# Weight tiles in one address class modulo 256 bytes, with the first MLP projection's weight parts at sixteen different distances from it

## The chip, the core and the metric

The kernel runs on one core of one Trainium2 chip. The metric is the time of one execution of the whole program in microseconds (us), measured on the device. The profile is of one such execution. Engines are named as in the profile: PE is the matrix engine (TensorE), PEld its weight loads, DVE the vector engine, ACT the scalar engine, POOL the GpSimd engine, SP the engine whose queue issues most of the loads.

## The reference

One layer of a decoder trunk on a sequence of 256 positions and a width of 2048, all in fp32:

```
h   = RMSNorm(x)
proj = h @ w_in                      # (256, 2048) @ (2048, 15376), split into branch inputs
oa  = gated delta rule               # branch A, 8 heads, chunks of 64
ob  = HGRN2 gated recurrence         # branch B, 8 heads
oc  = cross-attention into 256 memory tokens (mem_n @ w_kv_mem)   # branch C
merged = sum_b sigmoid(G_b h) * (o_b @ W_br_b)
x   = x + RMSNorm(merged @ w_out)
h2  = RMSNorm(x)
x   = x + RMSNorm(relu(h2 @ w_mlp_in)^2 @ w_mlp_out)              # width 8192 between
```

Most of the work is dense matrix products of 256 rows of activations with weights that are read once from HBM, 357 MB in all.

## The kernel before

**Split products.** fp32 accuracy is reached with a reduced fp32 type of the matrix engine (F32R): each operand is split into a high part and a low remainder, and a product becomes three: high by high, high by low, low by high. Weights arrive in 512 KB pieces of 256 rows by 512 columns (2 tiles of 128 rows, `KG = 2`); in each SBUF partition a piece is 4096 bytes. ACT copies a piece into a high part (`wh` or `oh`), DVE subtracts to give the low part (`wl` or `ol`), and PE uses both. ACT and DVE therefore do one instruction of about 1.05 and 1.22 us per piece, and PE reads every weight from where these two wrote it.

**Two ways to multiply.** In a *plain unit* (`unit`, and the products of `seven`) the activations are the stationary operand (128 columns are loaded into the array) and the weights are the moving one: for each 128-row tile and each of two halves of the positions there are three matmuls of 512 columns, which move `wh`, `wl`, `wh`. In a row of the profile such a matmul is `mm<-wl,hh`: first the moving tile, then the stationary one. In a *stacked unit* (`unit_stacked`, for all of the first MLP projection but its first unit; `unit_joined` in the layer's first part) the weights are stationary in blocks of 128 columns, and the activations move: a wide matmul moves 512 columns (high and low activations side by side) past the high weights, a narrow one moves 256 columns past the low weights (`mm<-h2h,oh` and `mm<-h2h,ol`). A stacked unit takes its 8 pieces two at a time: 16 wide and 16 narrow matmuls for each two, in alternating order; 64 and 64 in all.

**Where the tiles lie.** Until the end of `w_out` the weights come from the pool `wp`: four buffers each for the raw piece, for `wh` (4096 bytes each) and for `wl` (4224 bytes each, that is 128 more than 4096). After that, in the MLP, `pair_at` makes six pairs `oh0`/`ol0` to `oh5`/`ol5`, with `oh` of 4096 and `ol` of 4224 bytes, and `operand` hands them out in turn. The helper `low` places the low part in its tile, 16 floats (64 bytes) from the start where `aside` is true, which it is in the joined and stacked units.

Call a tile's byte address in its partition modulo 256 its *class*. All activations that PE reads in the products of weights (`hh`, `h2h`, `memT`, `mh`, `ml`, `sh`, `sl`, `mgh`, ...) lie in class 128. So do all `wh`. The `wl` of `wp` alternate between 128 and 0 from buffer to buffer, since 4224 is 16.5 times 256; in joined units, with their 64 bytes, between 192 and 64. The pairs of the MLP alternate too: `oh0`, `oh2`, `oh4` with their `ol` lie in class 128, `oh1`, `oh3`, `oh5` with theirs in class 0; the low parts of stacked units lie 64 bytes on, in classes 192 and 64. In this document the *distance* is the class of the weight minus the class of the activation, which is always 128: it is 0 or 128 for most tiles, and 64 or 192 (that is, minus 64) for the low parts of joined and stacked units.

**What sets the order.** Instructions are issued in the order of the code on each engine, with background steps of other branches put between groups by `tick`. The MLP runs over `e` from 0 to 7: a projection `mlp_in(e)` of two units (`u` 0 and 1, `c0 = e * 1024 + u * 512`, so `c0 // 512` counts the sixteen units), then `mlp_out(e - 1)`, which uses seven products in place of eight (`seven`) and two plain units; `mlp_out_last` ends the kernel with four plain units.

Of the kernel before, what the change touches and what calls it, by code (L numbers as in the profile page):

```python
# [11 lines left out]
F32R = mybir.dt.float32r  # L12
# [5 lines left out]
P = 128  # L18
# [15 lines left out]
KG = 2  # L34
# [6 lines left out]
def tile_trunk(ctx: ExitStack, tc, a):  # L41
# [44 lines left out]
    wp = weights.enter_context(tc.tile_pool(name="wp", bufs=4, side="right"))  # L86
# [3 lines left out]
    def nm(s):  # L90
        cnt[0] += 1
        return f"{s}_{cnt[0]}"

    def g4(name, shape=(P, 1024), dt=F32):
        return gp.tile(list(shape), dt, tag="g", name=nm(name))
# [11 lines left out]
    def bank(name):  # L107
        return pbp.tile([P, 512], F32, tag="bp", name=nm(name))
# [79 lines left out]
    def tick(share=1.0):  # L188
        credit[0] += rate[0] * share
        n = int(credit[0])  # L190
        credit[0] -= n
        pump(n)
# [9 lines left out]
            ))  # L202
        return w

    def low(t, aside):
        o = 16 if aside else 0
        return t[:, o:o + KG * 512].rearrange("p (k n) -> p k n", k=KG)

    def split_w(w, n, width=512, step=None, q=lambda i: i, home=None, aside=False):
        if home:  # L210
            wh, wl = home(aside)
        else:
            wh = wp.tile([P, KG, 512], F32R, tag="wh", name=nm("wh"))
            wl = low(wp.tile([P, KG * 512 + 32], F32R, tag="wl", name=nm("wl")), aside)
        for j in range(0, n, step or n):
            js = slice(j, min(j + (step or n), n))
            q(A.copy(wh[:, js, 0:width], w[:, js, 0:width]))
            q(V.tensor_tensor(out=wl[:, js, 0:width], in0=w[:, js, 0:width],
                              in1=wh.bitcast(F32)[:, js, 0:width], op=ALU.subtract))
        return wh, wl  # L220
# [36 lines left out]
    def products_joined(ps, groups, nk, cs, turned):  # L257

        for wide in (0, 1) if turned else (1, 0):
            for k0, (wh, wl), both in groups:
                for c in cs:
                    for j in range(KG):
                        end = k0 + j == nk - 1 and wide == turned
                        if wide:
                            T.matmul(ps[c], wh[:, j, c * P:(c + 1) * P], both[j], start=k0 + j == 0, stop=end)
                        else:
                            T.matmul(ps[c][:, 0:S], wl[:, j, c * P:(c + 1) * P], both[j][:, 0:S], start=False, stop=end)  # L270
                yield

    def flat(b):
        return b.rearrange("p s n -> p (s n)")

    def unit_stacked(pairs, nk, src, c0, ps, load, ws):

        for gg in range(0, nk // KG, 2):
            groups = []
            for g in (gg, gg + 1):  # L280
                k0 = g * KG
                groups.append((k0, ws[g] if g in ws else load(src, k0, c0, True),
                               [flat(pairs[kt // 4][:, kt % 4]) for kt in range(k0, k0 + KG)]))
            for i, _ in enumerate(products_joined(ps, groups, nk, range(4), gg // 2 % 2)):
                tick(0.5)
# [75 lines left out]
    def load_mem(g):  # L361

        c, half = g // 2, g % 2
        memB.append(g4("memT", (P, 2, 2, S), F32R))
        if half == 0:
            mem_s.append(g4("mem", (P, NT, 512)))
        if c < 2:
            sl = slice(half * 256, half * 256 + 256)
        elif half == 0:
            sl = slice(0, 512)  # L370
        else:
            return
        pin(nc.sync.dma_start(mem_s[c][:, :, sl], mem_r[:, :, c * 512 + sl.start:c * 512 + sl.stop]))
# [7 lines left out]
    def first_unit(src, c0):  # L381


        both = pmm.tile([P, 1024], F32, tag="mm", name=nm("mm"))
        ng = KT // KG
        ws, sw = {}, {}

        def fetch(g):
            load_mem(g)
            ws[g] = load_w_raw(src, g * KG, KG, c0, step=1 if g < 2 else None, q=pin)  # L390

        def piece(g, js, q=lambda i: i):
            if g not in sw:
                sw[g] = (wp.tile([P, KG, 512], F32R, tag="wh", name=nm("wh")),
                         low(wp.tile([P, KG * 512 + 32], F32R, tag="wl", name=nm("wl")), False))
            wh, wl = sw[g]
            q(A.copy(wh[:, js, :], ws[g][:, js, :]))
            q(V.tensor_tensor(out=wl[:, js, :], in0=ws[g][:, js, :], in1=wh.bitcast(F32)[:, js, :], op=ALU.subtract))

        def turn(g):  # L400
            parts = []
            for kt in (g * KG, g * KG + 1):
                pt, kk = bank("tr"), kt % 4
                for t in range(NT):
                    pin(T.transpose(pt[:, t * P:(t + 1) * P], mem_s[g // 2][:, t, kk * P:(kk + 1) * P], ident))
                parts.append((pt[:, 0:S], *mem_act(kt), gcol[:, kt:kt + 1]))
            return parts

        def products(kt):
            ah, al = mem_act(kt)  # L410
            wh, wl = sw[kt // KG]
            j = kt % KG
            ts = [slice(t * P, (t + 1) * P) for t in range(NT)]
            os = [both[:, t * 512:(t + 1) * 512] for t in range(NT)]
            for o, t in zip(os, ts):
                pin(T.matmul(o, ah[:, t], wh[:, j, :], start=kt == 0, stop=False))
                pin(T.matmul(o, al[:, t], wh[:, j, :], start=False, stop=False))
            for o, t in zip(os, ts):
                pin(T.matmul(o, ah[:, t], wl[:, j, :], start=False, stop=kt == KT - 1))

        fetch(0)
        fetch(1)
        idle_turns(11)
        turn_grow(grow_mem, 16, 0, pin)
        split_scaled(turn(0), pin)
        idle_turns(8)
        for j in range(KG):
            piece(0, slice(j, j + 1), pin)
        for g in range(ng):
            if 1 <= g < ng - 1:  # L430
                piece(g + 1, slice(0, KG))
            if g + 2 < ng:
                fetch(g + 2)
            products(g * KG)
            if g == 0:
                for j, part in enumerate(turn(1)):
                    split_scaled([part], pin)
                    piece(1, slice(j, j + 1), pin)
            elif g + 1 < ng:
                split_scaled(turn(g + 1))  # L440
            products(g * KG + 1)
            if g % 2 == 0 and g > 0:
                sumsq_chunk(mem_s[g // 2 - 1], ssm, g // 2 - 1)
            tick()
        sumsq_chunk(mem_s[3], ssm, 3)
        return both
# [851 lines left out]
    for hg in range(2):  # L1298
        k, g = forget(unit_joined(hboth, w_in, OFF_BF + 512 * hg), hg)
        q = unit_joined(hboth, w_in, OFF_BQ + 512 * hg)  # L1300
# [75 lines left out]
    ahead = {}  # L1376

    def first_weights(ps):
        for g in range(2):
            ahead[g] = load_w(a["w_mlp_in"][0], g * KG, KG, 0,  # L1380
                              home=lambda aside: tuple(g4(n, (P, KG, 512), F32R) for n in ("wh", "wl")))

    for c in range(4):
        ys.append(g4("y1", (P, NT, 512)))
# [37 lines left out]
    def at(pool, tag, dt):  # L1422
        return pool.tile([P, KG, 512], dt, tag=tag, name=tag, bufs=1)

    def pair_at(pool, i):
        return at(pool, f"oh{i}", F32R), pool.tile([P, KG * 512 + 32], F32R, tag=f"ol{i}", name=f"ol{i}", bufs=1)

    pairs = [pair_at(wx, i) for i in range(2)]
    raws = [at(wx, "raw0", F32)]

    def wide_ring():
        for g in range(2):
            w = load_w_raw(a["w_mlp_in"][0], g * KG, KG, 512)
            ahead[8 + g] = split_w(w, KG, home=operand, aside=True)
        weights.close()
        wy = ctx.enter_context(tc.tile_pool(name="wy", bufs=1, side="right", reuse_waits="tile"))
        raws.extend(at(wy, f"raw{i}", F32) for i in range(1, 5))
        raws.append(g4("raw5", (P, KG, 512)))
        pairs.extend(pair_at(wy, i) for i in range(2, 6))

    def operand(aside):
        pairs.append(pairs.pop(0))
        return pairs[-1][0], low(pairs[-1][1], aside)

    def raw(src, k0, c0):
        w = raws.pop(0)
        raws.append(w)
        nc.sync.dma_start(w, src[k0 * P:(k0 + KG) * P, c0:c0 + 512].rearrange("(k p) n -> p k n", p=P))
        return w

    def load_in(src, k0, c0, aside=False):
        return split_w(raw(src, k0, c0), KG, home=operand, aside=aside)

    h2act = act_of(h2T)
    stf = const("stf", [P, 8])
# [240 lines left out]
```

## Time and profile before

| | |
|---|---|
| time, median of 3 runs (range) | 1783.41 us (1782.7 to 1784.26) |
| the profiled execution's own time | 1783.16 us |
| its span, first to last instruction | 1781.4 us |
| PE busy | 1767.7 us, 99% of the span |
| DVE busy | 1302.8 us, 73% |
| ACT busy | 961.1 us, 54% |
| granted PE clock | 0.999 |
| DMA | 362.84 MB, 204 GB/s mean |

The program has 8841 matmul instructions, and the trace shows a record for each (9053, since some plain fp32 matmuls run in two passes). Matmuls are pipelined: one that moves 512 columns has a record of about 0.39 us, but the next starts some 0.23 us later. So the time that PE needs for a stretch of work is read from the starts of its rows, not from their durations. The page's mean duration in a row of PE is not its pace.

The MLP begins at about 1101 us of the span. From there stages of the first projection (two units, 44.1 us) and of the second (41.6 to 43.2 us) alternate; the last second projection runs from 1687 to 1773 us.

### The profile page before, as it was taken

The numbers are of one execution on the slowest core, as the hardware profiler recorded it, in microseconds if no ns is written. First come the engines' busy times: TensorE is split into PE (matmuls) and PEld (weight loads), VectorE is DVE, ScalarE is ACT, GpSimd is POOL, SyncE is SP. The second block draws the span as 40 slices with busy tenths as digits, with TensorE's granted clock in tenths as the row PEclk, the third lists the DMA queues.
The fourth block names the chain that finished last, engine by engine and source line by source line (L and its number), as shares of the span: only waits on it lengthen the run. The fifth ranks groups of instructions, "written<-read, shape, count | busy, mean of one in ns | idle before, by whom it ended". The sixth has DMA issues, their size and how long they took to land.

```text
span 1781.4 us, 23962 instructions
## 1 busy us (share of the span) xinstructions
PE 1767.7 (99%) x9053; PEld 1491.5 (84%) x9053; DVE 1302.8 (73%) x1764; ACT 961.1 (54%) x1217; POOL 57.8 (3%) x100
## 2 busy tenths in 40 slices
PE   9999999999999999999999999999999999999998
PEld 7888888888888888888888888888888878888886
DVE  6865768684758487697555557796979797969795
ACT  7645666454555475565444445665545464646453
POOL 0000000400030000000000000000000000000000
PEclk9999999999999999999999999999999999999999
DMA  8665555865487465555666665776767676767683
GB/s 272 206 194 166 175 156 166 232 205 156 154 215 213 130 195 166 156 171 174 183 186 192 233 224 197 231 244 217 245 222 252 206 245 217 256 200 257 204 298 139
DMA packets 188804, 362.84 MB, mean 204 GB/s; under 512 B 14456, under 2 KB 16272, under 8 KB 188304
## 3 DMA queue, kind: packets, MB, share of 16 engines
q1 hardware_dynamic: 181856, 351.32, 61.9%
q0 software_dynamic: 2304, 5.44, 1.6%
q10 hardware_dynamic: 4528, 4.54, 0.9%
q8 instruction: 71, 1.16, 0.3%
q14 instruction: 45, 0.37, 0.1%
HBM read 356.86 MB, written 4.39 MB: 203 GB/s over the span
## 4 chain that ended last, share of the span: by engine, by line
PE 81%; DVE 2%; issue 1%; ACT 1%; DMA 0%; DVEq 0%; POOLq 0%; POOL 0%
PE mm L56 77%; DVE ol L56 1%; PE pa L56 1%; PE kk L56 0%; DMA raw<-in_w_mlp_out 0%; DVE relu L56 0%; PE bo L56 0%; PE o L56 0%; PE pzt L56 0%; PE pw L56 0%; PE tr L56 0%; DVE raw L56 0%; DVE ml L56 0%; PE y L56 0%; PE mgT L56 0%
## 5 line engine op out<-in xcount | busy, mean ns | idle before, releaser
L56 DVE TENSOR_TENSOR wl<-w,wh 128x1024 fp32r<-128x1024 f32 (+1 forms) x362 | 436.8, 1217 | 238.2 <-ACT wh L56 215.8
L56 ACT CAST wh<-w 128x1024 fp32r<-128x1024 f32 (+1 forms) x362 | 374.7, 1045 | 357.9 <-PE mm L56 293.3
L56 ACT CAST oh<-raw 128x1024 fp32r<-128x1024 f32 x288 | 299.1, 1051 | 278.2 <-PE mm L56 213.8
L56 DVE TENSOR_TENSOR ol<-raw,oh 128x1024 fp32r<-128x1024 f32 x288 | 342.9, 1219 | 98.5 <-ACT oh L56 66.2
L56 PE MATMUL mm<-wh,hh 128*128 128x512 f32 x1152 | 366.6, 393 | 0.0
L56 PEld LDWEIGHTS mm<-wh,hh 128*128 128x128 f32 x1152 | 216.0, 188 | 46.3 <-ACT wh L56 0.2
L56 PE MATMUL mm<-h2h,oh 128*128 128x512 f32 x960 | 227.7, 393 | 0.0
L56 PE MATMUL mm<-wl,hh 128*128 128x512 f32 x576 | 226.1, 392 | 0.0
L56 PEld LDWEIGHTS mm<-h2h,oh 128*128 128x128 f32 x960 | 178.5, 188 | 38.2
L56 PE MATMUL mm<-hh,wh 128*128 128x512 f32 x768 | 184.8, 392 | 0.7 <-ACT z L56 0.7
L56 PEld LDWEIGHTS mm<-hh,wh 128*128 128x128 f32 x768 | 140.6, 188 | 28.3 <-ACT z L56 0.9
L56 PE MATMUL mm<-ol,mh 128*128 128x512 f32 x372 | 146.4, 393 | 1.1 <-DVE ol L56 1.0
L56 PE MATMUL mm<-oh,mh 128*128 128x512 f32 x372 | 146.2, 393 | 0.0
L56 PE MATMUL mm<-oh,ml 128*128 128x512 f32 x372 | 145.2, 393 | 0.0
L56 PEld LDWEIGHTS mm<-wl,hh 128*128 128x128 f32 x576 | 108.3, 188 | 21.4
L56 PEld LDWEIGHTS mm<-h2h,ol 128*128 128x128 f32 x960 | 113.7, 188 | 3.2 <-DVE ol L56 0.7
L56 PE MATMUL mm<-h2h,ol 128*128 128x256 f32 x960 | 114.6, 277 | 0.5 <-DVE ol L56 0.5
L56 PEld LDWEIGHTS mm<-hh,wl 128*128 128x128 f32 x768 | 97.0, 188 | 3.4
L56 PE MATMUL mm<-hh,wl 128*128 128x256 f32 x768 | 99.6, 280 | 0.0
L56 PEld LDWEIGHTS mm<-ol,mh 128*128 128x128 f32 x372 | 69.9, 188 | 18.5 <-DVE ol L56 2.8
L56 PEld LDWEIGHTS mm<-oh,mh 128*128 128x128 f32 x372 | 69.9, 188 | 16.6 <-DVE acc L56 1.1
L56 PEld LDWEIGHTS mm<-oh,ml 128*128 128x128 f32 x372 | 69.8, 188 | 15.7
(363 smaller groups left out, 2208.2 us busy)
## 6 DMA issues: line engine op xcount, KB each, us to landing
w<-in_w_in SPq DMA_DIRECT2D x240, 512.0 KB, 4.2
raw<-in_w_mlp_out SPq DMA_DIRECT2D x170, 512.0 KB, 4.6
raw<-in_w_mlp_in SPq DMA_DIRECT2D x118, 512.0 KB, 4.8
w<-in_w_out SPq DMA_DIRECT2D x32, 512.0 KB, 4.3
w<-in_w_kv_mem SPq DMA_DIRECT2D x30, 512.0 KB, 4.7
w<-in_w_br_c SPq DMA_DIRECT2D x16, 512.0 KB, 3.6
w<-in_w_br_a SPq DMA_DIRECT2D x16, 512.0 KB, 4.4
w<-in_w_br_b SPq DMA_DIRECT2D x16, 512.0 KB, 3.6
```

The costliest lines, as they stand in the source:

```text
L56: ins = op(*args, **kwargs)
```

## The change

The instructions, their order on every engine, their waits and the DMAs are the same in both programs. Only addresses in SBUF differ.

- In `wp` a low part that isn't aside is moved by 32 floats (128 bytes) in every second buffer. All `wl` of plain units then lie in class 128, like `wh` and the activations: distance 0. The low parts of joined units stay where they were (classes 192 and 64).
- The tiles of the MLP's pairs are 4352 bytes (17 times 256) for both parts, so all twelve lie in class 128. In `mlp_out` and `mlp_out_last`, where no place is given, all parts are at distance 0.
- In the stacked units of the first projection each unit takes its own pair of shifts from `places`, in floats, for the high and the low part. Unit 0 isn't stacked and takes none. In bytes (high, low), for units 1 to 15: (0, 128), (32, 32), (224, 224), (16, 96), (240, 160), (8, 16), (248, 240), (4, 8), (252, 248), (48, 48), (208, 208), (0, 192), (0, 64), (0, 4), (0, 0). Read modulo 256, 224 is minus 32, 240 minus 16, and so on.
- The pools `wx` and `wy` grow by 128 to 256 bytes per tile, so raw tiles lie at other addresses, all still in class 128.

```diff
-    def low(t, aside):
-        o = 16 if aside else 0
+    def shifted(t, o):
         return t[:, o:o + KG * 512].rearrange("p (k n) -> p k n", k=KG)
 
+    low_turn = [0]
+
+    def low(aside):
+        t = wp.tile([P, KG * 512 + 32], F32R, tag="wl", name=nm("wl"))
+        odd = low_turn[0] % 2
+        low_turn[0] += 1
+        return shifted(t, 16 if aside else 32 * odd)
...
+    places = [(0, 0), (0, 32), (8, 8), (56, 56), (4, 24), (60, 40), (2, 4), (62, 60),
+              (1, 2), (63, 62), (12, 12), (52, 52), (0, 48), (0, 16), (0, 1), (0, 0)]
+
     def unit_stacked(pairs, nk, src, c0, ps, load, ws):
...
-                groups.append((k0, ws[g] if g in ws else load(src, k0, c0, True),
+                groups.append((k0, ws[g] if g in ws else load(src, k0, c0, places[c0 // 512]),
...
     def pair_at(pool, i):
-        return at(pool, f"oh{i}", F32R), pool.tile([P, KG * 512 + 32], F32R, tag=f"ol{i}", name=f"ol{i}", bufs=1)
+        return tuple(pool.tile([P, KG * 512 + 64], F32R, tag=f"{t}{i}", name=f"{t}{i}", bufs=1) for t in ("oh", "ol"))
...
-            ahead[8 + g] = split_w(w, KG, home=operand, aside=True)
+            ahead[8 + g] = split_w(w, KG, home=operand, place=places[1])
...
-    def operand(aside):
+    def operand(place):
         pairs.append(pairs.pop(0))
-        return pairs[-1][0], low(pairs[-1][1], aside)
+        return tuple(shifted(t, o) for t, o in zip(pairs[-1], place))
...
-    def load_in(src, k0, c0, aside=False):
-        return split_w(raw(src, k0, c0), KG, home=operand, aside=aside)
+    def load_in(src, k0, c0, place=None):
+        return split_w(raw(src, k0, c0), KG, home=operand, place=place)
```

More of the change, by code (lines that the diff above doesn't have):

```diff
@@ L203, in load_w_raw, with split_w @@
         return w
-    def low(t, aside):
-        o = 16 if aside else 0
+    def shifted(t, o):
         return t[:, o:o + KG * 512].rearrange("p (k n) -> p k n", k=KG)
-    def split_w(w, n, width=512, step=None, q=lambda i: i, home=None, aside=False):
+    low_turn = [0]
[4 more added lines that the diff above has]
+        return shifted(t, 16 if aside else 32 * odd)
+    def split_w(w, n, width=512, step=None, q=lambda i: i, home=None, aside=False, place=None):
         if home:
-            wh, wl = home(aside)
+            wh, wl = home(place or (0, 16 if aside else 0))
         else:
             wh = wp.tile([P, KG, 512], F32R, tag="wh", name=nm("wh"))
-            wl = low(wp.tile([P, KG * 512 + 32], F32R, tag="wl", name=nm("wl")), aside)
+            wl = low(aside)
         for j in range(0, n, step or n):
@@ L394, in piece @@
                 sw[g] = (wp.tile([P, KG, 512], F32R, tag="wh", name=nm("wh")),
-                         low(wp.tile([P, KG * 512 + 32], F32R, tag="wl", name=nm("wl")), False))
+                         low(False))
             wh, wl = sw[g]
@@ L1380, in first_weights @@
             ahead[g] = load_w(a["w_mlp_in"][0], g * KG, KG, 0,
-                              home=lambda aside: tuple(g4(n, (P, KG, 512), F32R) for n in ("wh", "wl")))
+                              home=lambda place: tuple(g4(n, (P, KG, 512), F32R) for n in ("wh", "wl")))
     for c in range(4):
```

## Prediction, made before the change was run

> **What bounds the kernel now.** I read the page's busy times first, then the chain of waits from the start of the MLP on.
>
> ```profile
> span 1781.4 us, 23962 instructions
> PE 1767.7 (99%) x9053; PEld 1491.5 (84%) x9053; DVE 1302.8 (73%) x1764; ACT 961.1 (54%) x1217; POOL 57.8 (3%) x100
> by line: PE mm L56 90.3%; DVE ol L56 3.4%; issue 2.2%; DMA raw<-in_w_mlp_out 1.2%; DVE relu L56 1.1%; DVE raw L56 0.6%; DVE ml L56 0.5%; ACT oh L56 0.4%; ACT junk L56 0.1%; DVE yacc L56 0.1%; PE mT L56 0.1%; POOL rsf L1622 0.1%; ACT relu L5
> ```
>
> PE is the bound nearly everywhere; in the MLP a few per cent of the chain go through DVE. A change that alters no instruction can only act through how fast the same instructions run, so I went to the timeline of PE and took the pace from the starts of rows. The tile in a row was matched with its address in the built program.
>
> The second projection, in its last stage, where the weights move (`oh`, `ol` first) past activations at class 128. The first ten matmuls read a pair in class 128, the next twelve one in class 0, the last twelve one in class 128 again:
>
> ```profile
> 1734.60 0.39 PE L56 MATMUL mm<-oh,ml 128*128 128x512 f32 x1
> ...
> 1736.87 0.40 PE L56 MATMUL mm<-oh,mh 128*128 128x512 f32 x1
> ...
> 1739.66 0.39 PE L56 MATMUL mm<-oh,mh 128*128 128x512 f32 x1
> 1739.89 0.40 PE L56 MATMUL mm<-ol,mh 128*128 128x512 f32 x1
> 1740.12 0.39 PE L56 MATMUL mm<-oh,ml 128*128 128x512 f32 x1
> 1740.36 0.39 PE L56 MATMUL mm<-oh,mh 128*128 128x512 f32 x1
> ...
> 1742.39 0.40 PE L56 MATMUL mm<-oh,mh 128*128 128x512 f32 x1
> ```
>
> Ten matmuls take 2.27 us, 227 ns each, at distance 0. Twelve take 2.79 us, 232.5 ns each, at distance 128. Then three take 0.70 us (233 ns) and the next nine 2.03 us (226 ns): after a disturbance the pace comes back within a few matmuls. So a wide matmul at distance 128 costs 5.5 to 6 ns more than one at distance 0.
>
> A plain unit of `w_out`: a group of twelve with its low part in class 0, then a group with it in class 128.
>
> ```profile
> 1007.37 0.39 PE L56 MATMUL mm<-wh,mgh 128*128 128x512 f32 x1
> 1007.60 0.40 PE L56 MATMUL mm<-wl,mgh 128*128 128x512 f32 x1
> 1007.83 0.39 PE L56 MATMUL mm<-wh,mgl 128*128 128x512 f32 x1
> ...
> 1010.12 0.39 PE L56 MATMUL mm<-wh,mgh 128*128 128x512 f32 x1
> ...
> 1012.84 0.39 PE L56 MATMUL mm<-wh,mgh 128*128 128x512 f32 x1
> ```
>
> The first takes 2.75 us, the second 2.72: four of the twelve move a low part, so each costs about 7 ns more in class 0.
>
> The first projection, from the middle of one of its stages; equal matmuls follow each other there, so their rows merge:
>
> ```profile
> 1560.69 3.80 PE L56 MATMUL mm<-h2h,ol 128*128 128x256 f32 x32
> 1564.32 7.55 PE L56 MATMUL mm<-h2h,oh 128*128 128x512 f32 x32
> 1571.71 3.80 PE L56 MATMUL mm<-h2h,ol 128*128 128x256 f32 x32
> ```
>
> 32 narrow ones take 3.63 us, 113.4 ns each, half of 226.8: at distances 64 and 192 they run clean. 32 wide ones take 7.39 us, 230.9 ns each, 4.2 above 226.7: half of them have their weights at distance 128. A narrow matmul at distance 0 is seen only elsewhere, in the attention's scores, where all operands lie in class 128:
>
> ```profile
> 169.76 0.28 PE L56 MATMUL sc<-ckh,cqh 128*128 128x256 f32 x1
> ...
> 171.20 0.63 PE L56 MATMUL mm<-hh,wh 128*128 128x512 f32 x2
> ```
>
> Twelve take 1.44 us, 120 ns each: for a narrow matmul distance 0 is the bad place, by 6.6 ns.
>
> One page bears on why wide and narrow differ. The Trainium skill (TensorE: Matmul & The Clock Gate, LDWEIGHTS) gives the time of a weight load in ns as its columns divided by 1.2, so 107 ns for 128 columns; by that, as an estimate, a load nearly fills a narrow matmul's 113 ns and any delay to it shows, while under a wide one it has 120 ns to spare. The 113 and 120 ns agree with that; they don't prove it.
>
> **The change part by part.** The sum is made against the profiled execution, 1783.16 us with a span of 1781.4, 0.25 us under the median of 1783.41.
>
> *Plain units.* The low parts that move, from the groups by line:
>
> ```profile
> L56 PE MATMUL mm<-wl,hh 128*128 128x512 f32 x576 | 226.1, 392 | 0.0
> L56 PE MATMUL mm<-wl,oh 128*128 128x512 f32 x128 | 50.3, 393 | 0.2 <-DVE wl L56 0.2
> L56 PE MATMUL mm<-wl,mgh 128*128 128x512 f32 x128 | 50.2, 392 | 0.0
> L56 PE MATMUL mm<-wl,och 128*128 128x512 f32 x64 | 25.1, 392 | 0.0
> L56 PE MATMUL mm<-wl,memT 128*128 128x512 f32 x64 | 22.6, 394 | 0.0
> ```
>
> These are 960, half of them in class 0: 480 x 7 ns = 3.4 us. Some of these matmuls stand at waits for ACT or DVE, where a faster pace only waits longer, so I take 3.1. The bounds are 2.5 and 3.8 (the clean matmuls after a disturbed one gain a little too).
>
> *Second projection.* Its matmuls and the stage that shows its other limit, the first columns of the second row being the stretch, its length and PE's busy time, the third busy time DVE's:
>
> ```profile
> L56 PE MATMUL mm<-oh,mh 128*128 128x512 f32 x372 | 146.2, 393 | 0.0
> L56 PE MATMUL mm<-oh,sh 128*128 128x512 f32 x112 | 44.6, 399 | 0.2 <-DVE relu L56 0.2
> 1428.04:1471.27 43.23, 42.37 (x182) 33.41 (x180) 41.61 (x46) 25.95 (x27) 0.00 (x0) 1.00 0.70 234
> 1687.12:1773.00 85.88, 85.88 (x373) 69.57 (x371) 69.42 (x82) 40.51 (x50) 0.54 (x1) 1.00 0.60 215
> ```
>
> Three products for each row make 3 x (372 + 112) = 1452 matmuls, half at distance 128: 726 x 5.9 ns = 4.3 us, and the three slow ones after each change of class about 0.4 more: 4.7. But in the six stages before the last, DVE is busy 41.6 of 43.2 us and PE waits there for it; what PE saves ahead of such a wait is given back in it. Each stage would save some 0.55 us, and about half of that comes ahead of its last wait: 5 x 0.28 = 1.4 lost. The last stage has no wait and keeps its 1.4. I take 3.3, with bounds 2.0 (every earlier stage held by DVE) and 4.7.
>
> *First projection.* 15 stacked units of 64 wide and 64 narrow. Now each costs 64 x 4.2 ns = 0.27 us above the clean pace, narrow ones next to nothing: 4.2 us in all. Afterwards every wide matmul stands at 0 or within 48 bytes of it, and no narrow one is sure of its clean place. No row shows a distance that isn't a multiple of 64, so I bound and interpolate. Wide: 0.3 ns (distance 0) to 5.8 (distance 128), on a straight line 1.2 ns at the ten units' mean distance of 22 bytes, 0.08 us a unit. Narrow: 6.6 ns at 0 and none at 64, so about 6 at 4 and 8 bytes, 5 at 16, 3.3 at 32 (and at 96, 128, taken as midway to the unknown), 1.6 at 48; over the ten units with both parts shifted 3.8 on average, 0.25 us a unit. Ten units cost 3.3 us. Of the five others two (low at 64 and 192) are clean; the three with low at 128, 4 and 0 cost 3.3, 6.3 and 6.6 ns x 64, together 1.0. Sum 4.4 against 4.2: 0.2 us lost. Bounds: 1.0 if shifts cost nothing beyond those three (a gain of 3.2), and 17.9 + 1.1 if every matmul of the ten units loses 14 ns, the most that the rows suggest, twice a low part's 7 ns (a loss of 14.8). DVE and ACT don't hold these stages: DVE's writes and reads at shifted addresses cost as before where `ol` already stands 64 bytes on.
>
> ```profile
> 1297.55:1341.64 44.09, 44.09 (x257) 38.66 (x256) 30.83 (x31) 19.53 (x24) 0.00 (x0) 1.00 0.66 214
> L56 DVE TENSOR_TENSOR wl<-w,wh 128x1024 fp32r<-128x1024 f32 (+1 forms) x362 | 436.8, 1217 | 238.2 <-ACT wh L56 215.8
> L56 DVE TENSOR_TENSOR ol<-raw,oh 128x1024 fp32r<-128x1024 f32 x288 | 342.9, 1219 | 98.5 <-ACT oh L56 66.2
> ```
>
> PE fills this stage to the end, DVE has 13 of 44 us free; that is the cover, and with it gone a shift that slowed DVE by 43% would set the stage.
>
> Joined units are untouched. Sum: 1783.16 - 3.1 - 3.3 + 0.2 = 1777.0 us.
>
> **The rivals.**
>
> *The odd distances eat the gain.* Every matmul of the ten shifted units loses 7 ns, wide and narrow: 10 x 128 x 7 = 9.0, with the three low parts 10.1, so 5.9 more than now against 6.4 saved: 1782.7. For it: 7 ns is the step that both kinds of matmul show. Against: wide matmuls find their pace again by themselves at distance 0, and a small shift is a small phase.
>
> *The odd distances cost more than all else saves.* A weight block shifted by 4 to 48 bytes collides with the activations' reads on every load, twice over, and the wide matmuls never settle: 14 ns on each of the 1280 matmuls, 14.8 us lost, 1783.16 - 6.4 + 14.8 = 1791.6. It decides from (6.4 + 4.2 - 1.1 + 3.6) / 1280 = 10.2 ns each. Nothing in the trace shows such a place, nor excludes it.
>
> *The small shifts are free.* Narrow and wide run clean at all but the worst places: 3.2 gained in the first projection, 1773.6.
>
> *DVE takes the second projection's gain.* If each of the six earlier stages is set by DVE, 2.0 us of the 3.3 remain, and with narrow matmuls at 6.6 ns in all ten units the first projection loses 2.1: 1783.16 - 3.1 - 2.0 + 2.1 = 1780.2, at the edge of no change.
>
> *Addresses don't matter.* The time stays at 1783.2; the differences by class would be of something that goes with the buffer, such as the phase of the loads. Against it stand the rows of two kinds of unit with the same step. The Trainium skill (SBUF — State Buffer, SBUF: two separate sides) says that among engines only the port pair of DVE and GpSimd contends and that PE waits on nobody; by that rule the change would do nothing. The rows above, 227 against 232.5 ns, speak against it for PE's own two reads.
>
> **How the numbers follow.** Forecast 0.45; small shifts free 0.13; shifts eat the gain 0.19; DVE takes it 0.07; addresses don't matter 0.03; shifts cost more 0.13. A difference of 0.2%, 3.6 us, is about what a measurement of this kernel tells from none. Faster by more than that: 0.45 + 0.13 = 0.58. Within it: 0.19 + 0.07 + 0.03 = 0.29. Slower: 0.13. The predicted time is that of the forecast, 1777.0. Its own range, from the bounds of plain units and second projection and a first projection between -1.5 and +2.5, is 1773.5 to 1780.5. The range for 8 in 10 goes from 1772.5, below the free case, over the two cases of no change to 1786, and leaves out most of the last case.
>
> **What would show it.** In the profile after, groups of twelve in plain units should all take 2.72 us, and the last second projection should fall from 85.9 to about 84.5 us: if not, the class isn't the cause. The stage at 1428 us should shorten by less than 0.55 us and DVE's waits grow: that shows the give-back. In the first projection the unit with shifts (0, 64) should run 64 wide matmuls at 226.7 ns and 64 narrow at 113.3, and the one with (0, 0) its narrow ones at 120. The ten others decide the result: I am wrong on the slow side if their wide matmuls run above 234 ns, or narrow ones above 120, and on the fast side if both stay at the clean pace.

## The result and the profile after

| | before | after |
|---|---|---|
| median of the runs on the same chip (range), us | 1784.25 (1782.7 to 1785.66) | 1780.45 (1779.05 to 1781.7) |
| profiled execution, us | 1783.16 | 1781.33 |
| its span, us | 1781.4 | 1779.6 |
| first part, to the start of the MLP, us | 1100.03 | 1097.81 |
| seven stages of the first projection, us | 332.73 | 336.67 |
| seven stages of the second projection, us | 338.60 | 335.03 |

The change makes the kernel faster by 0.22%, 3.8 us by the medians: the ratio is 0.9978, with a 95% interval of 0.9971 to 0.9985. The forecast, 1777.0 us, stood 6.2 us below the profiled execution that it was summed from. The two profiled executions differ by only 1.83 us, since that of before was among the faster of its kernel and that of after among the slower; the parts below are compared between these two, and the timed runs of single parts (further down) show the same balance.

The page of after, busy times:

```profile
span 1779.6 us, 23962 instructions
PE 1764.0 (99%) x9053; PEld 1495.0 (84%) x9053; DVE 1302.7 (73%) x1764; ACT 961.4 (54%) x1217; POOL 58.8 (3%) x100
L56 PE MATMUL mm<-h2h,ol 128*128 128x256 f32 x960 | 119.0, 281 | 0.4 <-DVE ol L56 0.4
```

The same row of the narrow matmuls on the page of before:

```profile
L56 PE MATMUL mm<-h2h,ol 128*128 128x256 f32 x960 | 114.6, 277 | 0.5 <-DVE ol L56 0.5
```

PE is still the bound, with 3.7 us less to do, although 960 narrow matmuls got 4.4 us dearer. Where that shows is told by the busy times in stretches of the MLP. First before: the first row is the first part, then the sum of the first projection's stages, then that of the second's (stretch, its length, then busy times; in a sum, the sum of the lengths first):

```profile
1.64:1101.67 1100.03, 1098.27 (x5673) 929.60 (x5674) 751.36 (x1180) 599.28 (x792) 55.76 (x88) 1.00 0.63 189
...
sum 332.73, PE 332.19 PEld 290.92 DVE 235.58 ACT 160.29 POOL 0.00; mean PE 47.46 PEld 41.56 DVE 33.65 ACT 22.90 POOL 0.00
...
sum 338.60, PE 337.23 PEld 270.93 DVE 311.46 ACT 200.39 POOL 0.54; mean PE 48.18 PEld 38.70 DVE 44.49 ACT 28.63 POOL 0.08
```

And after, with three stages whose rows before the prediction shows: one of the first projection, an early one of the second, and the last:

```profile
1.65:1099.46 1097.81, 1094.70 (x5674) 929.44 (x5674) 751.28 (x1180) 599.86 (x792) 56.68 (x88) 1.00 0.63 190
...
1296.91:1341.83 44.92, 44.92 (x258) 39.27 (x256) 31.52 (x31) 19.55 (x24) 0.00 (x0) 1.00 0.67 211
...
sum 336.67, PE 336.22 PEld 294.79 DVE 236.23 ACT 160.19 POOL 0.00; mean PE 48.03 PEld 42.11 DVE 33.75 ACT 22.88 POOL 0.00
...
1427.99:1469.73 41.74, 41.48 (x182) 33.55 (x180) 40.76 (x46) 26.04 (x27) 0.00 (x0) 1.00 0.73 242
...
1686.32:1771.16 84.84, 84.84 (x373) 69.48 (x371) 69.61 (x82) 40.48 (x51) 0.54 (x1) 1.00 0.62 217
...
sum 335.03, PE 333.11 PEld 270.78 DVE 310.83 ACT 200.23 POOL 0.54; mean PE 47.59 PEld 38.68 DVE 44.40 ACT 28.60 POOL 0.08
```

The first part gained 2.2 us and the second projection 3.6, as forecast in kind. The first projection, for which 0.2 us was allowed, lost 3.9: its stage of 44.09 us takes 44.92, and PE fills it in both. The three differences add up to -1.85 us; the spans differ by 1.8.

Plain units and the second projection now run at one pace. The timeline of PE after, twelve matmuls of a plain unit whose low part would have been in class 0, then twelve of the last second projection:

```profile
1005.54 0.39 PE L56 MATMUL mm<-wh,mgh 128*128 128x512 f32 x1
...
1008.26 0.39 PE L56 MATMUL mm<-wh,mgh 128*128 128x512 f32 x1
...
1724.76 0.39 PE L56 MATMUL mm<-oh,mh 128*128 128x512 f32 x1
...
1727.48 0.39 PE L56 MATMUL mm<-oh,mh 128*128 128x512 f32 x1
```

Both take 2.72 us, 227 ns a matmul; before there were groups of 2.75 and of 2.79.

The first projection after: unit 10 (48 and 48 bytes), unit 12 (0 and 192), unit 15 (0 and 0):

```profile
1477.25 7.63 PE L56 MATMUL mm<-h2h,oh 128*128 128x512 f32 x32
1484.72 3.95 PE L56 MATMUL mm<-h2h,ol 128*128 128x256 f32 x32
1488.50 7.60 PE L56 MATMUL mm<-h2h,oh 128*128 128x512 f32 x32
...
1563.29 7.46 PE L56 MATMUL mm<-h2h,oh 128*128 128x512 f32 x32
1570.59 3.93 PE L56 MATMUL mm<-h2h,ol 128*128 128x256 f32 x32
1574.36 7.46 PE L56 MATMUL mm<-h2h,oh 128*128 128x512 f32 x32
...
1667.72 4.00 PE L56 MATMUL mm<-h2h,ol 128*128 128x256 f32 x32
1671.56 7.44 PE L56 MATMUL mm<-h2h,oh 128*128 128x512 f32 x32
```

By the starts, unit 10 runs 32 wide ones in 7.47 us, 233.4 ns each, as slow as at distance 128. Unit 12 has settled wide ones, 7.30 us or 228.1 ns each, but its 32 narrow ones at 192 take 3.77 us, 117.8 ns each, where the prediction counted on 113.4. At distance 0 they take 3.84 us, 120.0 ns, as forecast. From the same kind of rows, all units (before, each had wide ones at 230.6 to 231.1, narrow ones at 113.5, and 0.28 to 0.31 us above the clean pace of 226.7 and 113.3; unit 1's waits are left out):

| unit: shifts in bytes | wide, ns | narrow, ns | above clean pace, us |
|---|---|---|---|
| 1: 0, 128 | 227.8 | 119.4 | 0.43 |
| 12: 0, 192 | 228.1 | 117.7 | 0.37 |
| 13: 0, 64 | 227.4 | 117.8 | 0.33 |
| 14: 0, 4 | 227.8 | 118.1 | 0.37 |
| 15: 0, 0 | 227.5 | 119.8 | 0.47 |
| 5: -16, 160 | 228.1 | 119.9 | 0.52 |
| 8 and 9: 4, 8 and -4, -8 | 232.4, 231.9 | 115.8, 117.6 | 0.52, 0.61 |
| 6 and 7: 8, 16 and -8, -16 | 230.8, 233.1 | 118.3, 119.5 | 0.59, 0.81 |
| 4: 16, 96 | 231.5 | 118.0 | 0.61 |
| 2 and 3: 32, 32 and -32, -32 | 233.0, 233.2 | 118.5, 117.3 | 0.74, 0.67 |
| 10 and 11: 48, 48 and -48, -48 | 233.3, 231.8 | 118.3, 116.8 | 0.74, 0.55 |

Together 8.3 us against 4.3 before: 4.0 more, which is the loss of the stages.

### The profile page after: what moved, and what is told of

Same layout as the page of the kernel before. It is cut to its first block, busy times and chain, and to the rows that moved or that the text cites. A ratio compares the mean times of both kernels' runs of the same rounds, so it can differ in the third digit from the quotient of the medians.

```text
span 1779.6 us, 23962 instructions
## 1 busy us (share of the span) xinstructions
PE 1764.0 (99%) x9053; PEld 1495.0 (84%) x9053; DVE 1302.7 (73%) x1764; ACT 961.4 (54%) x1217; POOL 58.8 (3%) x100
## 4 chain that ended last, share of the span: by engine, by line
PE 78%; DVE 4%; issue 1%; DMA 1%; ACT 1%; DVEq 0%; POOLq 0%; POOL 0%; ACTq 0%
PE mm L56 74%; DVE ol L56 2%; PE pa L56 1%; DMA raw<-in_w_mlp_out 1%; DVE relu L56 1%; DVE raw L56 1%; PE kk L56 0%; DVE ml L56 0%; PE bo L56 0%; PE o L56 0%; PE pzt L56 0%; PE pw L56 0%; PE tr L56 0%; PE y L56 0%; PE mgT L56 0%
## 5 line engine op out<-in xcount | busy, mean ns | idle before, releaser
L56 PEld LDWEIGHTS mm<-h2h,ol 128*128 128x128 f32 x960 | 117.7, 188 | 3.2 <-DVE ol L56 0.6
L56 PE MATMUL mm<-h2h,ol 128*128 128x256 f32 x960 | 119.0, 281 | 0.4 <-DVE ol L56 0.4
```

The lines of the kernel that those rows point to most:

```text
L56: ins = op(*args, **kwargs)
```

## The experiments

Two questions were open. Why do narrow matmuls at distances 64 and 192 no longer run clean? And what are the two gains worth by themselves? For the first, one theory says that the table's odd shifts, or what goes with them, are at fault, and a narrow matmul's pace follows from its own distance. The other says that the pace of a narrow matmul follows from the state in which the wide ones ahead of it leave the two streams of reads: wide ones that were still unsettled, at distance 128, let it run clean, and wide ones that had settled at distance 0 don't. (The traces show starts and addresses, not reads: that it is PE's reads that collide is how both theories picture it, and isn't shown.)

### One class for all, no table (e1_one_class)

The changed kernel with one place for every stacked unit, high part at 0 and low part at 64 bytes:

```diff
-    places = [(0, 0), (0, 32), (8, 8), (56, 56), (4, 24), (60, 40), (2, 4), (62, 60),
-              (1, 2), (63, 62), (12, 12), (52, 52), (0, 48), (0, 16), (0, 1), (0, 0)]
+    places = [(0, 16)] * 16
```

> The change without its table: every weight tile in the class of the activations, all stacked units with shifts (0, 64 bytes). Theory A (the distance of a matmul's own operands sets its pace): narrow matmuls stand at distance 64 as in half of the kernel before, so they run at 113.3 ns, the wide ones at 226.7 but for the first few; the fifteen stacked units lose 1.0 us against 4.3 before, and the kernel is some 3.3 + 3.1 + 3.3 = 9 to 10 us faster than before. Theory B (the pace hangs on the phase that the matmuls before leave; narrow ones run at 113 only when they follow wide ones that have not settled): narrow ones take 117.8 ns as in units 12 and 13 of the change, each unit loses 0.33 us, 5.0 in all, and the kernel is only 5 to 6 us faster than before.

Measured: 1778.88 us (1777.0 to 1779.17) against 1784.72, ratio 0.9963 (0.9949 to 0.9977). A stage of the first projection on its timeline, and the sum of the seven stages:

```profile
1118.47 7.44 PE L56 MATMUL mm<-h2h,oh 128*128 128x512 f32 x32
1125.75 3.93 PE L56 MATMUL mm<-h2h,ol 128*128 128x256 f32 x32
1129.52 7.44 PE L56 MATMUL mm<-h2h,oh 128*128 128x512 f32 x32
```

```profile
sum 333.35, PE 332.82 PEld 294.34 DVE 236.34 ACT 160.23 POOL 0.00; mean PE 47.55 PEld 42.05 DVE 33.76 ACT 22.89 POOL 0.00
```

With no odd shift anywhere, the wide ones run at 227.5 ns, and narrow ones at the very distance that was clean before take 3.77 us, 117.8 ns each. So the clean pace isn't a property of the distance alone. The first projection still stands 0.6 us above before, and the table costs 3.3 us more than a single place: without it the change would be worth some 6.6 us by this ratio (4.1 to 9.1), 5.8 by the medians.

### The last wide ones before each narrow run put at distance 128 (e4_unsettled)

As e1, but of a unit's eight pieces the second and the sixth have their high part moved by 128 bytes. Theirs are the wide matmuls just ahead of a run of narrow ones; all low parts stay at 64 bytes.

```diff
+    def place_of(g):
+        return (32 if g in (1, 5) else 0, 16)
...
-                groups.append((k0, ws[g] if g in ws else load(src, k0, c0, places[c0 // 512]),
+                groups.append((k0, ws[g] if g in ws else load(src, k0, c0, place_of(g)),
```

> As e1, but in each stacked unit the high parts of the second and sixth piece, after which narrow matmuls follow, stand at distance 128. Theory B: the wide matmuls of these two pieces take some 232.5 ns (0.05 us more for each piece), the narrow ones after them fall to 113.3 ns within four; a unit loses 0.15 to 0.18 us, 2.3 to 2.7 in all, and the kernel is 2.3 to 2.7 us faster than e1. Theory A: narrow ones run at the same pace as in e1, and the kernel is 1.4 us slower than e1.

Measured: 1777.19 us (1773.96 to 1778.68) against the runs of before, ratio 0.9951 (0.9939 to 0.9964), some 8.7 us faster than before by the ratio and 7.5 by the medians. The same stretch, and the sums of both projections:

```profile
1118.19 7.50 PE L56 MATMUL mm<-h2h,oh 128*128 128x512 f32 x32
1125.53 3.80 PE L56 MATMUL mm<-h2h,ol 128*128 128x256 f32 x32
1129.16 7.50 PE L56 MATMUL mm<-h2h,oh 128*128 128x512 f32 x32
```

```profile
sum 331.03, PE 330.54 PEld 290.80 DVE 236.02 ACT 160.09 POOL 0.00; mean PE 47.22 PEld 41.54 DVE 33.72 ACT 22.87 POOL 0.00
...
sum 334.91, PE 333.04 PEld 270.97 DVE 310.55 ACT 199.78 POOL 0.54; mean PE 47.58 PEld 38.71 DVE 44.36 ACT 28.54 POOL 0.08
```

Nothing about the narrow matmuls was changed, and they went from 117.8 to 113.4 ns (3.63 us for 32). The wide ones got slower by 1.9 ns (7.34 us for 32), and a unit stands 0.17 us above the clean pace, against 0.33. So what stands ahead of them sets their pace, as the theory of the state at entry has it, and the narrow one's own distance alone doesn't.

### Low parts at 64 and 192 in turn (e5_alternate)

The kernel before also had its low parts at 64 and 192 by turns. As e1, with that turn:

```diff
+    def place_of(g):
+        return (0, 48 if g % 2 else 16)
```

> As e1, but the low parts of the stacked units stand at distance 64 and 192 in turn from piece to piece, as in the kernel before; all wide matmuls at 0. It tells whether the turn between 64 and 192, and not the unsettled wide matmuls, kept narrow ones at 113 ns before. If the turn did it: narrow ones 113.4 ns throughout and 0.08 us above the clean pace for a unit. If the phase on entry does (theory B): narrow ones begin at 118 as in e1; as in the joined units, where the turn comes every four matmuls, a turn may shift the phase on the way, so 115 to 118 ns on average and 0.2 to 0.35 us for a unit.

A single execution gave 1779.85 us against 1784.86. Narrow ones stay at 117.8 ns:

```profile
1119.08 7.48 PE L56 MATMUL mm<-h2h,oh 128*128 128x512 f32 x32
1126.40 3.93 PE L56 MATMUL mm<-h2h,ol 128*128 128x256 f32 x32
1130.17 7.48 PE L56 MATMUL mm<-h2h,oh 128*128 128x512 f32 x32
```

A unit stands 0.41 us above the clean pace, more than in e1. The turn isn't what kept the narrow ones clean.

### Which shifts of the wide ones do it (e9_shift_scan)

As e4, but the shift of the second and sixth piece is 16 bytes times the unit's number, so that one run holds fifteen shifts:

```diff
+    def place_of(g, u):
+        return (4 * u if g in (1, 5) else 0, 16)
```

> As e4, but the high parts of the second and sixth piece of unit u stand at 16 u bytes (16, 32, ... 240) in place of 128, so one run shows fifteen shifts. Unit 8 repeats e4: wide ones of these pieces 232.5 ns, narrow ones after them 113.4, the unit 0.17 us above the clean pace. If any unsettled wide matmul frees the narrow ones, shifts whose wide matmuls run at 231 to 235 ns (32, 48, 208, 224 in the change) give narrow ones at 113 too; if only certain phases do, most give 115 to 120. A shift of 240, where wide matmuls took 228 ns, is the cheapest if it frees them: 0.11 us for a unit.

A single execution took 1777.44 us. Narrow ones by the shift of the wide ones ahead, in ns, from the starts of their rows:

| shift, bytes | 16 | 32, 48, 64 | 80 | 96 | 112 | 128 | 144 | 160 | 176 | 192 | 208 | 224, 240 |
|---|---|---|---|---|---|---|---|---|---|---|---|---|
| wide of the shifted pieces, ns | 226.6 | 232.2, 232.5, 233.4 | 231.9 | 234.7 | 233.1 | 232.6 | 226.6 | 233.1 | 230.2 | 229.4 | 231.6 | 233.0, 226.6 |
| narrow, ns | 117.8 | 117.8 | 113.4 | 114.0 | 117.8 | 113.5 | 117.8 | 113.7 | 113.3 | 113.7 | 113.4 | 117.8 |
| unit above clean pace, us | | 0.44 | 0.16 | 0.23 | 0.45 | 0.17 | 0.33 | 0.20 | 0.12 | 0.12 | 0.15 | 0.45, 0.33 |

At 16 bytes the values are those of unit 1's second half, since its first half holds waits. Two neighbouring units on the timeline, 128 bytes up to 1402 us and 144 from there on, with wide ones of 7.33 and 7.28 us for 32 and narrow ones behind them of 3.63 and 3.77:

```profile
1387.55 7.50 PE L56 MATMUL mm<-h2h,oh 128*128 128x512 f32 x32
1394.88 3.80 PE L56 MATMUL mm<-h2h,ol 128*128 128x256 f32 x32
1398.51 7.44 PE L56 MATMUL mm<-h2h,oh 128*128 128x512 f32 x32
1405.79 3.93 PE L56 MATMUL mm<-h2h,ol 128*128 128x256 f32 x32
1409.56 7.44 PE L56 MATMUL mm<-h2h,oh 128*128 128x512 f32 x32
```

The narrow pace takes one of two values, 113.4 or 117.8, apart from the first few of a run, which raise some means to 114.0. At 16, 144 and 240 bytes the shifted wide ones run clean, and the narrow ones behind them take 117.8, as the theory asks of settled ones. But not every unsettled wide run brings the better value: 32, 48, 64, 112 and 224 don't, though their wide ones take 232 to 233 ns, as at 128. So the theory needs a narrower wording: certain states at entry hold a narrow run at 113.4, and which shift leaves such a state isn't told by how slow the wide ones are. Why it is these shifts stays open. The scan shows the same of wide ones: 16 bytes cost them nothing here, where only two pieces of eight are shifted, and 4.8 ns in the change, where unit 4 stands there as a whole.

### The best of these shifts in all units (e10_phase_176)

As e4, with 176 bytes:

```diff
-        return (32 if g in (1, 5) else 0, 16)
+        return (44 if g in (1, 5) else 0, 16)
```

> The best shift of the scan: as e4, with the high parts of the second and sixth piece 176 bytes on in place of 128. Theory B, from the scan's unit 11: wide ones of these pieces at 230 ns, narrow ones after them 113.3 from the first, 0.12 us above the clean pace for a unit, 1.8 us in all. That is 0.7 us less than e4 and 5.8 less than the change in the first projection: 9 to 10 us faster than before. If the scan's value hung on what stood around unit 11: as e4, 8 to 9 us faster than before.

Measured: 1777.09 us (1776.25 to 1777.71) against 1784.86, ratio 0.9955 (0.9942 to 0.9969). The sums of the two projections:

```profile
sum 330.25, PE 329.70 PEld 290.06 DVE 234.65 ACT 160.19 POOL 0.00; mean PE 47.10 PEld 41.44 DVE 33.52 ACT 22.88 POOL 0.00
...
sum 336.93, PE 333.86 PEld 270.50 DVE 311.96 ACT 200.33 POOL 0.54; mean PE 47.69 PEld 38.64 DVE 44.57 ACT 28.62 POOL 0.08
```

The first projection is 0.8 us shorter than in e4, a unit 0.12 us above the clean pace. But in this profiled execution the second is 2.0 us longer, and PE was busy for only 0.8 of that: the rest are waits. e4 and e10 can't be told apart in time. Both are faster than the kernel before, and by a narrow margin faster than the change: their intervals of the ratio, each against the kernel before on the same chip, end at 0.9964 and 0.9969, where that of the change begins at 0.9971.

### The second projection's part alone (e2_second_only)

The kernel before, with all pairs of the MLP in class 128 and the stacked units' parts moved back to the classes that they had:

```diff
+        i, oh, ol = pairs[-1]
+        o = 32 * (i % 2) if aside else 0
+        return shifted(oh, o), shifted(ol, o + 16 if aside else 0)
-        return pairs[-1][0], low(pairs[-1][1], aside)
```

> Only the second projection's weights are put into the activations' class; stacked units (distance 0 and 128, low parts at 64 and 192) and plain units of the first part as before. Forecast's term: 3.3 us faster than before. If DVE gives back all that PE saves in the six stages that it nearly fills: 1.4 to 2.0 us. If it gives back nothing: 4.7 us.

Measured: 1781.07 us, ratio 0.9980 (0.9971 to 0.9989), some 3.6 us. The narrow ones of the first projection stay at 113.5 ns.

### The plain units' part alone (e3_plain_only)

The kernel before, with only the low parts of the first part's plain units in class 128:

```diff
+        odd = low_turn[0] % 2
+        low_turn[0] += 1
+        return shifted(t, 16 if aside else 32 * odd)
```

> Only the low parts of the plain units before the MLP are put into the activations' class; the MLP as before. Forecast's term: 3.1 us faster than before. If waits for ACT and DVE take back what the trace of the change shows (waits 1.1 us longer in this part): 2.0 to 2.4 us. If the class does nothing here: no change.

Measured: 1781.32 us, ratio 0.9979 (0.9970 to 0.9988), some 3.7 us. Its first part:

```profile
1.64:1098.85 1097.21, 1095.09 (x5673) 930.20 (x5674) 751.18 (x1180) 599.96 (x792) 56.52 (x88) 1.00 0.63 190
```

That is 2.8 us less than in the profiled execution of before. The length of this part differs between executions of equal instructions and addresses, by its waits: it is 1100.0 to 1102.9 us in four with the addresses of before (before, e2, e7, e8) and 1096.2 to 1097.8 in seven with those of the change. PE's busy time in it differs less: 1098.3 to 1098.8 us in the four, 1094.7 in the change and 1095.1 in e3.

The two parts together are 7.3 us; take off e1's 0.6 in the first projection and there are 6.7, where e1 measured about 6.6 by its ratio; take off the change's 3.9 and there are 3.4, where it measured 3.8. The sum of the parts holds as far as these runs can tell, each part being known to about 1.6 us.

### DVE's share in the second projection (e7_no_sums and e8_second_no_sums)

The kernel before (e7) and e2 (e8), each without the four additions of weights by which DVE prepares the seven products, in the six earlier stages:

```diff
-            add_w(w22, w22, w12)
-            add_w(w12, w12, w11)
             product(6, w22, d)
-            add_w(w11, w22, w11)
             product(4, w12, d)
-            add_w(w21, w11, w21)
```

> The kernel before without the four additions of weights per half of the seven products (they are left out, so DVE has some 10 us less to do in each stage of the second projection). If DVE holds PE there: the waits in the six earlier stages go (0.15 to 1.8 us each before) and each takes 41.5 us, that is 40.8 at the clean pace and 0.7 for distance 128. If the waits have another cause, they stay.

> As e7, with the second projection's weights in the activations' class: each of the six earlier stages takes 40.9 us, 0.6 less than in e7, and the last 84.2 to 84.5 against 85.5 to 85.9: without DVE's load the whole 4.7 us of the second projection arrive. If PE's pace there is not what the class changes, both kernels have equal stages.

The products of these stages then work on weights that weren't summed. e7 took 1782.76 us and e8 1776.4, a single execution each. Busy times of e7: an early stage, the last one, and the sum:

```profile
1429.67:1471.32 41.65, 41.65 (x182) 33.64 (x181) 37.81 (x43) 26.05 (x27) 0.00 (x0) 1.00 0.75 242
...
1686.73:1772.60 85.87, 85.87 (x373) 69.58 (x371) 66.03 (x79) 40.53 (x50) 0.54 (x1) 1.00 0.60 215
...
sum 335.34, PE 335.34 PEld 271.40 DVE 288.05 ACT 201.04 POOL 0.54; mean PE 47.91 PEld 38.77 DVE 41.15 ACT 28.72 POOL 0.08
```

The same of e8:

```profile
1426.02:1467.21 41.19, 41.19 (x181) 33.64 (x180) 37.61 (x43) 26.22 (x27) 0.00 (x0) 1.00 0.74 245
...
1681.62:1766.24 84.62, 84.62 (x373) 69.57 (x371) 65.95 (x79) 40.50 (x50) 0.54 (x1) 1.00 0.62 218
...
sum 331.14, PE 331.14 PEld 271.38 DVE 287.18 ACT 201.32 POOL 0.54; mean PE 47.31 PEld 38.77 DVE 41.03 ACT 28.76 POOL 0.08
```

In both PE fills every stage, so this is the gain with no give-back: 4.2 us, 0.46 in the early stage and 1.25 in the last. Of the 6.4 us between the two executions 2.1 lie in the first part, where both programs are the same. With the additions in place the change got 3.57, so DVE kept about 0.6 us in this pair of executions. That figure is loose. With the second projection's addresses as in the change, the six earlier stages together take from 250.2 us (the change) to 253.7 (e2, whose profiled execution is the slowest of its eleven), 251.5 in the mean of seven; with those of before they take 252.7 and 253.6 (e3). The means differ by 1.7 us, where e7 and e8 differ by 2.95 in these stages: by that, DVE kept 1.3.

e7 also shows that DVE's load isn't what sets the pace in the first projection: the last six of its seven stages take 44.09 to 44.10 us each, as before, though DVE is busy for only 24.2 to 25.4 us of them in place of 29.8 to 31.5.

### Everything moved by 128 bytes (e6_gap)

The kernel before with an unused tile of 128 bytes per partition ahead of the pools with the activations. They go to class 0. The weights of the first part and four of the MLP's six pairs stay, so that their distances turn by 128; the first two pairs move along with the activations and keep theirs.

```diff
     cst = ctx.enter_context(tc.tile_pool(name="cst", bufs=1))
+    cst.tile([P, 32], F32, tag="gap", name="gap")
```

> The kernel before with one unused tile of 128 bytes ahead of the activations' pools: activations move from class 128 to class 0, the weights' pool in the layer's first part stays where it was. If the distance decides: all high parts of the plain units (some 1770 matmuls) and the stationary high parts of the joined units (900) now stand at distance 128 and lose 6.5 and 5.7 ns each: 13 to 17 us slower than before, in the plain units 12 matmuls in 2.79 us or more. In the MLP the first two pairs move along and the other four do not, so as many weights as before stand at distance 128 and its stages stay as they were. If the weights' own address decides: no change.

Measured: 1796.33 us against 1784.8, ratio 1.0063 (1.0040 to 1.0086), 11.2 to 11.5 us slower by ratio and medians. The two groups of a plain unit on its timeline, and its first part:

```profile
1005.53 0.40 PE L56 MATMUL mm<-wh,mgh 128*128 128x512 f32 x1
...
1008.30 0.39 PE L56 MATMUL mm<-wh,mgh 128*128 128x512 f32 x1
...
1011.08 0.40 PE L56 MATMUL mm<-wh,mgh 128*128 128x512 f32 x1
```

```profile
1.65:1112.19 1110.54, 1109.29 (x5674) 930.47 (x5674) 752.25 (x1180) 598.97 (x792) 56.53 (x88) 1.00 0.62 188
```

Groups of 2.77 and 2.78 us stand where there were 2.72 and 2.75, and the first part takes 10.5 us more with the same instructions. In the regular stretch of the last second projection the roles are exchanged: pairs in class 0 now run nearly clean (0 to 15 ns in twelve matmuls above the clean pace), those in class 128 don't (71 to 80 ns; both by the starts of rows, where before it was 11 to 15 and 71 to 75 the other way round). So it is the distance of weight from activation that counts, not the class of the weight. The expectation was 13 to 17 us. One place where it falls short is the plain units: by the starts of their rows, their groups of twelve stand 52 and 62 ns above the clean pace, the second below the 71 ns of twelve times 5.9.

## Why the prediction was right and wrong

- **Plain units (-3.1): right.** Summed over the starts of PE's rows, the excess over the clean pace in the first part fell from 10.3 to 6.9 us, by 3.4, the price worked out before anything was taken off for waits; 1.1 us came back as waits in this profiled execution, though executions with one set of addresses differ in their waits by more than that. The part alone measured 3.7 us, so the 0.3 taken off for waits can't be told from nothing.
- **Second projection (-3.3): right in sum.** It measured 3.57, and 3.6 alone (e2). The gain in full was put at 4.7 and is 4.2 by e7 and e8, somewhat less; the give-back was put at 1.4, and the runs leave it between 0.6 and 1.3. The last stage fell by 1.04, not by 1.4. The stage at 1428 us shortened by 1.49, more than the 0.55 that was given as a sign, and PE's waits in it shrank where they were to grow: before, it held 0.86 us of them, after 0.26, and in e7, with distances as before, it takes 41.65 us without any. So that one stage was no sign of the give-back.
- **First projection (+0.2): this step failed**, with 3.9, inside its outer bounds of -3.2 to +14.8 but above the +2.5 that the forecast's own range allowed it. What it cost before was right (4.2 forecast, 4.3 measured). What it costs after was put at 4.4 and is 8.3. That the pace goes with the distance was right (e6, e8); that a matmul's own distance is enough to tell it was not, and the term was mis-sized at three places.
  - *Wide ones at small shifts, 1.2 ns each on a straight line from 0 to 128.* They cost 5.2 on average (231.9 ns in the ten units), nearly the 5.5 to 6 of distance 128. 4.0 ns times 640 matmuls are 2.6 us: the main miss. Distance doesn't act in proportion: 4 bytes cost 5.7 ns, and -16 bytes 1.4.
  - *Narrow ones in those units, 3.8 ns on average.* They cost 4.7: another 0.6 us.
  - *Narrow ones of units 12 and 13, counted as clean because rows at 64 and 192 were clean.* They cost 4.4 ns. Those rows had been taken behind wide matmuls half of which stood at distance 128, which the change itself took away; e1, e4 and e5 show that this was what kept them clean. With what the other three units and the settled wide ones cost above the 1.0 allowed, the five units came to 2.0 us.
- **The total.** 1780.45 us lies at the very edge of the forecast's own range, 1773.5 to 1780.5, and that it lies inside is in part luck: the first projection's term left its part of that range by 1.4 us, while plain units and second projection alone gained 0.9 more than was taken for them (3.7 and 3.6 for 3.1 and 3.3). The bounds that the range was made from add up to 1773.2 to 1781.2. The range for 8 in 10, up to 1786, holds "no change" too, so a time inside it says little about the mechanism.
- **The rivals.** "The odd distances eat the gain" had the right kind of loss: each of the ten units costs 0.64 us on average where it allowed 0.9 (128 times 7 ns). The time lies between it (1782.7) and the forecast (1777.0): nearer to the rival as it stands, nearer to the forecast as a difference from before (3.8 us, where the forecast stands for 6.2 and the rival for 0.5). "DVE takes the second projection's gain" comes to nearly the measured time, 1780.2, but by the wrong way: it has the second projection gain 2.0 us where it gained 3.6, and the first lose 2.1 where it lost 3.9. "Addresses don't matter" is excluded by e6. The Trainium skill (SBUF — State Buffer, SBUF: two separate sides), by which PE never waits on anyone, and by which, as the prediction read it, nothing should have moved, differs from the 11 us that 128 unused bytes cost there; the measurement decides.
- **The signs named in advance.** The groups of twelve at 2.72 us, the last stage (84.84 us for about 84.5) and the narrow ones of the unit at (0, 0), 119.8 ns for 120, came out as named. The unit at (0, 64) did not: 117.8 ns for 113.3. Those on the slow side, wide above 234 ns or narrow above 120, did not come true though the first projection's term missed: together they are 9.0 us (7.3 and 6.7 ns on 640 matmuls each), and the ten units lost 6.3 without reaching either.

## What to carry to other kernels

A pace that is read from a row belongs to that row among its neighbours: before using it for a changed program, ask what ran ahead of it and whether the change leaves that in place. Where PE is the bound, compare the starts of equal matmuls by their operands' addresses modulo 256 bytes (the change's tiles, 17 times 256 bytes long, all stand in one class, and in the last second projection they all run at the clean pace); a class for all weights that equals that of the activations was worth 6 to 7 us of 1784 here (e1), and an unused 128 bytes ahead of them cost 11. Between two known points of such an effect a straight line was no estimate here; a scan of one parameter over equal units of one run shows its course at the price of a single run, as long as one asks again whether a value found there holds when all units take it (e10).

## What was not expected of the hardware

- **Two values for narrow matmuls.** A run of 32 at distances 64 or 192 takes 113.4 or 117.8 ns each in the mean, by what ran ahead of it (e4 and e1). At distance 0 it takes 120.0.
- **The price of a shift isn't monotonic.** Wide matmuls run at 227.5 ns at shift 0, at 228.1 at -16 bytes, and at 231 to 233 at all other shifts of the table from 4 to 48 bytes either way. With only two pieces of eight shifted by 16 bytes they run at 226.6 (e9). In e9, neighbouring shifts of 112, 128 and 144 bytes bring narrow ones of 117.8, 113.5 and 117.8 ns.
- **It is the sum of the program that decides.** e4 slows 16 of the 64 wide matmuls of a unit (232.6 ns for 226.6), and its first projection is 2.3 us shorter than e1's. In time the two can't be told apart: the medians differ by 1.7 us (1777.19 against 1778.88), and the intervals of their ratios overlap.
- Not tried: the joined units of the first part, whose narrow matmuls stand at 118 and 113 ns by turns and whose buffers have no room for a shift; and why certain states at entry hold the narrow pace at 113.4.
